# Attention stage of a two-layer diffusion trunk: four softmax divisions moved to another engine, one set of splits queued earlier, and the closing of a head placed between its transposes

## The chip, the cores and the metric

The kernel runs on one core of one Trainium2 chip. A core has four compute engines that the text names by short names: PE (TensorE, matrix products and transposes), DVE (VectorE), ACT (ScalarE) and POOL (GpSimd); PEld is PE's weight load, SP is the engine whose queue issues most of the DMA transfers. Each engine works through its own instructions in the order in which they stand, and waits at an instruction until the semaphores that it names have come. The metric is the device time of one execution in microseconds (us), the median over several executions; lower is better.

## The reference

The reference is a trunk of two layers over 1024 latent tokens and 256 context tokens, with 1024 channels. The part that matters here is layer 0, whose mixer has two groups of heads side by side: eight attention heads (two key/value heads, head size 64) and four HGRN heads (a gated linear recurrence in both directions). In short:

```
def attend(q, k, v):                       # per block of queries
    s = einsum("bqhgd,bkhd->bhgqk", q, k) * ATTN_SCALE
    p = softmax(s, axis=-1)
    return einsum("bhgqk,bkhd->bqhgd", p, v)
# latent queries: keys = 256 context + 1024 latent; context queries: the 256 context keys only
y = concat([attention heads, rms_norm(hgrn out) * silu(gate)], -1) @ w_out
x = x + g1 * rms_norm(y, norm_post_mix)
```

After it come the first ConvFFN, the second layer (neighbourhood attention) and the second ConvFFN; none of them is touched by the change.

## The kernel before, in words

The whole program is one list of instructions for each engine. Within the attention stage (`even_attention`, L1110) the order on every engine, SP included, is the order in which the code issues the work.

**Blocks, pairs and steps.** Queries are taken in five blocks of 256: block 0 is the context (`blocks` in `even_attention`), blocks 1 to 4 are the latent tokens. A pair is one block and one of eight heads, so there are 40 pairs: 0 to 7 for the context, 8 to 39 for the latent tokens. Each pair has two query tiles of 128. The loop at L1359 makes 88 steps `s`; the text calls a step even or odd by `s`. For the pair p a tile's scores are made in steps 2p and 2p+1, its exponential and its division one step later, its transposes in steps 2p+4 and 2p+5, its product with the values in steps 2p+6 and 2p+7, and its closing (`finish`) in step 2p+7. So in one step several pairs are at work, each at another place.

**One step on the engines.** PE makes the scores into the PSUM tile `a_s` (one buffer); DVE copies them, negated, into `l_p` with the row's minimum (L1179; `c_p` for the context); ACT takes the exponential in place and sums it (L1186). The division is DVE's reciprocal `rl` (L1191) and a multiplication by it on POOL (L1192). Then the probabilities are transposed on PE into `a_pt` (two buffers, `tp`), five key tiles to a step, in three pieces: two of 128x512 and a last one of 128x256. From each piece ACT makes the high half `a_ph` (L1213) and DVE the low half `a_pl` (L1214). PE multiplies both halves with the values into `a_pv` (one buffer, ten products to a step). The closing adds the two halves of `a_pv`: ACT copies the upper one to `pv_t` (L1249), DVE adds the lower one into `a_oT` (L1251). The next pair's products go into the same `a_pv`, so they wait for that addition.

**Filler.** Beside this PE has the output projection (`project`, L1280), cut into parts of three products (`g_ps<-w_h,a_oh` and so on). The function `step(n)` gives out n parts; a step of the loop calls it twice, between the pieces of the transposes. Every part also issues one item of the list `late`: the squares and copies of a finished projection tile, its norm, its residual, its stores. A block's 32 parts may only be given out once `st["ready"]` has reached the block; otherwise `step` only issues a waiting item of `late`, and PE has no filler. A block needs its attention output and its four HGRN tiles split into high and low halves (`split`, L1238: ACT makes `a_oh`, POOL makes `a_ol`). The list `todo` holds those splits; the end of each step takes some of them, one and a third of what is there. `gated` (L1261) first gives out what is left of the previous block's parts.

**The HGRN tiles.** They were stored to memory (`hgd`) by POOL's queue and are read again by SP's queue into `a_g`, four transfers to a block. The read is issued at the closing of the head 5 of the same block, in the buffer `r0` or `r1`.

**The first values.** The context's pairs use other PSUM tiles for their product: `h_pd` for pairs 0 to 2, then `a_s` for pairs 1 and 3 where the stage's own PSUM pool is already open (only pair 3 meets this), `g_ps` for pairs 5 and 7, and `a_pv` for the others. `a_s` lies over the banks that `h_pd` had.

Of the kernel before, what the change touches and what calls it, by code (L numbers as in the profile page):

```python
# [20 lines left out]
P = 128  # L21
# [47 lines left out]
class Trunk:  # L69
# [1040 lines left out]
    def even_attention(self, gp, tp, pp1, sp, more):  # L1110
# [77 lines left out]
        def divide(i):  # L1188
            Pt, nm, nk = st["t", i]
            rl = self.small.tile([P, 1], F32, name="rl")  # L1190
            nc.vector.reciprocal(rl, st.pop(("l", i)))  # L1191
            nc.gpsimd.tensor_scalar(Pt[:, :nk], Pt[:, :nk], rl, None, op0=OP.mult)  # L1192

        def half_keys(pair, half):

# [21 lines left out]
        def values(pair, half):  # L1217
            b, h = pairs[pair]
            kts = half_keys(pair, half)
            if half == 0:  # L1220
                pp = more.get("pp")
                if not pp:
                    st["pv"] = pp1.tile([P, 2, 5, 32], F32, name=f"h_pd{pair % 2}", bufs=1).rearrange("p a b c -> p (a b c)")
                elif pair in (1, 3):
                    st["pv"] = pp.tile([P, NT * P], F32, name="a_s", bufs=1)[:, :512]
                elif pair in (5, 7):
                    st["pv"] = gp.tile([P, 512], F32, name="g_ps")
                else:
                    st["pv"] = pp.tile([P, 512], F32, name="a_pv", bufs=1)
            pv, g = st["pv"], h // (AQ // AKV)  # L1230
            last = not half_keys(pair, 1) if half == 0 else True
            for j, kt in enumerate(kts):
                v = V2[keys(b)[0] // P + kt][:, g * P:(g + 1) * P]
                for x in range(2):
                    self.mm(pv[:, :QB], v, st["p", half][x][:, j], half == 0 and j == 0 and x == 0,
                            last and j == len(kts) - 1 and x == 1)
# [6 lines left out]
        def finish(pair):  # L1243
            b, h = pairs[pair]
            pv = st["pv"]
            if h % 2 == 0:
                st["oT"] = sp.tile([P, QB], F32, name="a_oT", bufs=2)
            t = pv_t[64:128]
            nc.scalar.copy(t, pv[64:128, :QB])  # L1249
            r = 64 * (h % 2)  # L1250
            nc.vector.tensor_tensor(out=st["oT"][r:r + 64], in0=pv[0:64, :QB], in1=t, op=OP.add)  # L1251
            if h % 2 == 1:
                todo.append(lambda oT=st["oT"]: split(b, h // 2, oT))
            if h == AQ - 3:
                g = st["g", b] = self.wp.tile([P, BH, QB], F32, name="a_g", tag=f"r{b % 2}")
                for k in range(BH):
                    nc.sync.dma_start(g[:, k, :], self.hgd[k][:, blocks[b][0]:blocks[b][0] + QB])
            if h == AQ - 1:
                todo.extend(lambda k=k: gated(b, k) for k in range(BH))

        def gated(b, k):  # L1261

            step(32 * b - at[0])
            split(b, BH + k, st["g", b][:, k, :])
            if k == BH - 1:
                st["ready"] = b

        def squares(y, ms):
            junk = sp.tile([P, 512], BF16, name="yjunk", bufs=1)
# [76 lines left out]
        load_values(NT - 2, NT)  # L1346
        load_q(2)
        load_ctx_keys(1)
        yield
        later = [lambda: load_keys(0, 0), lambda: load_keys(0, 1), lambda: load_values(0, NT - 2), lambda: load_keys(1, 0),  # L1350
                 lambda: load_keys(1, 1)] + [lambda m=m: load_w(m) for m in range(4)]
        for s in range(N + 8):
# [17 lines left out]
            step(1)  # L1370
            next(t, None)
            step(1)
            next(t, None)
            if 0 <= s - 1 < N:
                divide(s - 1)
            if 0 <= pair - 3 < len(pairs) and half == 1:
                finish(pair - 3)
            for _ in range(min(len(todo), 1 + len(todo) // 3)):
                todo.pop(0)()
            yield  # L1380
# [1590 lines left out]
```

## Time and profile before

| | |
|---|---|
| median of 3 executions | 3265.8 us (3262.59 to 3266.71) |
| profiled execution: its own time | 3258.97 us |
| profiled execution: span from first to last instruction | 3257.1 us |
| mean granted TensorE clock | 0.978 |
| PE busy over the span | 3065.0 us, 94% |
| DVE, ACT, POOL busy over the span | 66%, 46%, 48% |
| attention stage, latent scores to last transposes | about 640 to 990 us of the span |

The stage that the change touches is a ninth of the span. The shares over the whole span say little about it; what counts there is where PE stands idle inside a step, and which engine's instruction ends that idle time. A view by windows gives the busy time of each engine in a stretch; the timeline gives single instructions with the idle time before them in brackets and the instruction that ended it.

### The profile page before, as it was taken

Reading aid. Unit: us, or ns where it says so; the run is one execution under the profiler, and the core shown is the slowest. Engines: PE = TensorE matmul, PEld = TensorE weight load, DVE = VectorE, ACT = ScalarE, POOL = GpSimd, SP = SyncE. Lnnn points to the kernel's source line nnn. Section 1 sums busy time; section 2 is a strip of 40 time slices with the busy share of each in tenths; the row PEclk is TensorE's granted clock in tenths of the full one; section 3 lists DMA queues with packets and bytes.
Section 4 is the critical chain, followed back from the end, with each engine's and each line's share of the span. In section 5 each row is a group of like instructions: output and inputs, shape, how many; then the busy total and the mean of one; then the engine's idle time right before and its main releaser. Section 6 shows DMA issues by size and latency. Waiting matters only on the chain.

```text
span 3257.1 us, 48812 instructions
## 1 busy us (share of the span) xinstructions
PE 3065.0 (94%) x18161; PEld 2538.8 (78%) x18161; DVE 2147.4 (66%) x3619; ACT 1508.0 (46%) x2705; POOL 1576.6 (48%) x1165
## 2 busy tenths in 40 slices
PE   7989999789998899999999989999998989999999
PEld 4766777578876688888888768898986768888787
DVE  4556666677775787787678752577775464555787
ACT  3432332466665444334344442566665533443444
POOL 1130111377774677776600111677765367777300
PEclk8999999899999999999999989999998989999999
DMA  7734111711114344434365763222224212222755
GB/s 263 239 95 138 46 36 36 265 37 58 59 59 150 100 153 142 146 138 153 137 241 195 240 212 124 59 62 62 64 78 160 88 69 80 79 90 84 249 198 187
DMA packets 217142, 412.93 MB, mean 127 GB/s; under 512 B 25776, under 2 KB 87744, under 8 KB 216904
## 3 DMA queue, kind: packets, MB, share of 16 engines
q1 hardware_dynamic: 207208, 376.24, 34.5%
q0 software_dynamic: 9696, 33.57, 2.7%
q8 instruction: 143, 2.34, 0.3%
q14 instruction: 95, 0.78, 0.1%
HBM read 322.67 MB, written 87.44 MB: 126 GB/s over the span
## 4 chain that ended last, share of the span: by engine, by line
PE 76%; DVE 11%; issue 4%; ACT 3%; DMA 3%; POOL 2%; SPq 0%; POOLq 0%; ACTq 0%; DVEq 0%
PE g_ps L140 20%; PE u_g L140 14%; PE d_ps L140 12%; PE u_v L140 10%; PE u_pc L140 3%; PE a_pv L140 2%; PE c_pv L140 2%; PE c_s L140 2%; PE c_pt L2595 2%; PE a_pt L1212 2%; DVE a_pl L1214 1%; PE o_ps L140 1%; PE a_s L140 1%; DMA d_rawB<-in_w_down 1%; ACT a_ph L1213 1%
## 5 line engine op out<-in xcount | busy, mean ns | idle before, releaser
L148 POOL TENSOR_TENSOR rs_r<-rs_e,mhalf 128x1 f32<-128x1 f32 (+3 forms) x102 | 83.9, 824 | 833.6 <-DVE rs_e L147 466.2
L140 PE MATMUL d_ps<-d_Bl,d_Ah 128*128 128x512 f32 x704 | 276.5, 393 | 2.8 <-DVE d_Bl L1978 2.2
L2578 POOL TENSOR_SCALAR c_p<-c_p,rl 128x640 f32<-128x640 f32 (+1 forms) x128 | 232.6, 1818 | 94.6 <-DVE rl L2577 62.9
L140 PE MATMUL d_ps<-d_Bh,d_Ah 128*128 128x512 f32 x704 | 275.7, 392 | 2.4 <-ACT d_Ah L1977 1.4
L140 PE MATMUL d_ps<-d_Bh,d_Al 128*128 128x512 f32 x704 | 275.6, 391 | 1.5 <-DVE d_Al L1978 1.5
L140 PE MATMUL g_ps<-xh,w_hi 128*128 128x512 f32 (+1 forms) x640 | 256.7, 401 | 8.7 <-DVE hq L826 6.6
L1192 POOL TENSOR_SCALAR l_p<-l_p,rl 128x1280 f32<-128x1280 f32 x64 | 225.6, 3525 | 55.0 <-DVE rl L1191 48.8
L140 PE MATMUL g_ps<-xh,w_lo 128*128 128x512 f32 (+1 forms) x640 | 237.9, 372 | 1.2 <-POOL w_lo L2478 1.2
L140 PE MATMUL g_ps<-xl,w_hi 128*128 128x512 f32 (+1 forms) x640 | 237.7, 371 | 0.0
L1214 DVE TENSOR_TENSOR a_pl<-a_pt,a_ph 128x512 fp32r<-128x512 f32 (+1 forms) x200 | 119.0, 603 | 86.8 <-ACT a_ph L1213 86.3
L1653 DVE TENSOR_TENSOR f_u<-u_v,f_p 128x512 f32<-128x512 f32 x88 | 60.5, 687 | 156.6 <-PE u_v L140 156.6
L365 DVE CUSTOM_DVE_ANT_0 m_raw<-m_raw,c_row 128x512 f32<-128x512 f32 x128 | 147.0, 1158 | 24.8 <-DMA m_raw<-in_w_mod 24.8
L140 PEld LDWEIGHTS d_ps<-d_Bl,d_Ah 128*128 128x128 f32 x704 | 132.8, 189 | 34.2 <-DVE d_Bl L1978 5.5
L140 PEld LDWEIGHTS d_ps<-d_Bh,d_Ah 128*128 128x128 f32 x704 | 132.8, 189 | 31.9 <-ACT d_Ah L1977 2.6
L1639 POOL TENSOR_TENSOR w_S4l<-w_s,w_S4h 128x512 fp32r<-128x512 f32 x44 | 57.4, 1303 | 205.2 <-ACT w_S4h L1638 205.2
L140 PEld LDWEIGHTS d_ps<-d_Bh,d_Al 128*128 128x128 f32 x704 | 132.9, 189 | 30.1 <-DVE d_Al L1978 2.8
L2598 DVE TENSOR_TENSOR c_pl<-c_pt,c_ph 128x256 fp32r<-128x256 f32 (+1 forms) x256 | 113.1, 470 | 59.9 <-ACT c_ph L2597 58.7
L1213 ACT CAST a_ph<-a_pt 128x512 fp32r<-128x512 f32 (+1 forms) x200 | 101.9, 518 | 108.4 <-PE a_pt L1212 108.3
L140 PE MATMUL g_ps<-w_hi,xh 128*128 128x512 f32 (+1 forms) x368 | 143.4, 390 | 6.0 <-DVE xh L2352 3.4
L140 PEld LDWEIGHTS g_ps<-xh,w_hi 128*128 128x128 f32 x640 | 121.7, 190 | 27.8 <-issue 7.6
L140 PE MATMUL g_ps<-w_lo,xh 128*128 128x512 f32 (+1 forms) x368 | 138.2, 376 | 3.7 <-DVE w_lo L2339 2.6
L2597 ACT CAST c_ph<-c_pt 128x256 fp32r<-128x256 f32 (+1 forms) x256 | 98.4, 414 | 91.4 <-PE c_pt L2595 89.2
(602 smaller groups left out, 10018.6 us busy)
## 6 DMA issues: line engine op xcount, KB each, us to landing
w_raw<-in_w_up SPq DMA_DIRECT2D x88, 512.0 KB
d_rawA<-actd SPq DMA_DIRECT2D x77, 512.0 KB
d_rawB<-in_w_down SPq DMA_DIRECT2D x74, 512.0 KB
m_raw<-in_w_mod SPq DMA_DIRECT2D x128, 256.0 KB
m_raw<-in_w_mod SPq DMA_DIRECT2D x48, 512.0 KB
actd<-f_t SPq DMA_DIRECT2D x22, 640.0 KB
actd<-f_t SPq DMA_DIRECT2D x22, 512.0 KB
vcd<-cv_st POOLq DMA_DIRECT2D x20, 512.0 KB, 2.9
```

Source lines behind the costliest of these rows:

```text
L140: return self.nc.tensor.matmul(out, lhsT, rhs, start=start, stop=stop, skip_group_check=True, **k)
L148: nc.gpsimd.tensor_tensor(out=r[:p, :n], in0=e[:p, :n], in1=self.mhalf[:p, :n], op=OP.pow)
L365: nc.vector.tensor_tensor_reduce(out=w, in0=w, in1=halves[1][n % 2], scale=1.0, scalar=0.0, op0=OP.mult, op1=OP.add, accum_out=acc[:, k, o ...
L1192: nc.gpsimd.tensor_scalar(Pt[:, :nk], Pt[:, :nk], rl, None, op0=OP.mult)
L1212: nc.tensor.transpose(pt[:, m, qt * P:(qt + 1) * P], Pt[:, kts[j + m] * P:(kts[j + m] + 1) * P], self.ident)
L1213: nc.scalar.copy(ph[:, j:j + n], pt[:, :n])
L1214: nc.vector.tensor_tensor(out=pl[:, j:j + n], in0=pt[:, :n], in1=ph[:, j:j + n].bitcast(F32), op=OP.subtract)
L1653: nc.vector.tensor_tensor(out=out, in0=x, in1=y, op=OP.add)
L2578: nc.gpsimd.tensor_scalar(Pt[:, :n], Pt[:, :n], rl, None, op0=OP.mult)
L2595: nc.tensor.transpose(pt[:, j, :], Pt[:, (src + j) * P:(src + j + 1) * P], self.ident)
L2597: nc.scalar.copy(vap(ph, o, dims), pt[:, :cnt])
L2598: nc.vector.tensor_tensor(out=vap(pl, o, dims), in0=pt[:, :cnt], in1=vap(ph, o, dims).bitcast(F32), op=OP.subtract)
```

## The change

Four things are edited, all in `even_attention`.

1. In `divide`, the odd query tiles of pairs 8 to 11 (tile numbers 17, 19, 21 and 23) are multiplied by `rl` on ACT; the even ones stay on POOL.
2. In `values`, pair 3 uses `a_pv` as pair 4 does, and no longer `a_s`.
3. The HGRN tiles of a block are read one block earlier (`load_gated`): the context's before the loop, the block b+1's at the closing of head 5 of block b. For the context, the four HGRN splits are queued at the closing of head 4 instead of head 7. `ready` is set by an item of its own at the end of `todo`.
4. In the loop, `finish` comes after the second piece of the transposes and the filler behind it, before the third piece and the division; it came after both.

```diff
@@ divide
-            nc.gpsimd.tensor_scalar(Pt[:, :nk], Pt[:, :nk], rl, None, op0=OP.mult)
+            if 2 * AQ <= i < 3 * AQ and i % 2:
+                nc.scalar.mul(Pt[:, :nk], Pt[:, :nk], rl)
+            else:
+                nc.gpsimd.tensor_scalar(Pt[:, :nk], Pt[:, :nk], rl, None, op0=OP.mult)
@@ values
-                pp = more.get("pp")
-                if not pp:
+                if "pp" not in more:
...
-                elif pair in (1, 3):
-                    st["pv"] = pp.tile([P, NT * P], F32, name="a_s", bufs=1)[:, :512]
                 elif pair in (5, 7):
                     st["pv"] = gp.tile([P, 512], F32, name="g_ps")
                 else:
-                    st["pv"] = pp.tile([P, 512], F32, name="a_pv", bufs=1)
+                    st["pv"] = more["pp"].tile([P, 512], F32, name="a_pv", bufs=1)
@@ finish, load_gated, gated
             if h == AQ - 3:
+                load_gated(b + 1)
+            if (b, h) == (0, AQ - 4):
+                todo.extend(lambda k=k: gated(b, k) for k in range(BH))
+            if h == AQ - 1:
+                if b:
+                    todo.extend(lambda k=k: gated(b, k) for k in range(BH))
+                todo.append(lambda: st.update(ready=b))
+
+        def load_gated(b):
+            if b < len(blocks):
                 g = st["g", b] = self.wp.tile([P, BH, QB], F32, name="a_g", tag=f"r{b % 2}")
                 for k in range(BH):
                     nc.sync.dma_start(g[:, k, :], self.hgd[k][:, blocks[b][0]:blocks[b][0] + QB])
-            if h == AQ - 1:
-                todo.extend(lambda k=k: gated(b, k) for k in range(BH))
...
             split(b, BH + k, st["g", b][:, k, :])
-            if k == BH - 1:
-                st["ready"] = b
@@ before the loop
         load_ctx_keys(1)
+        load_gated(0)
         yield
@@ the loop
             step(1)
+            if 0 <= pair - 3 < len(pairs) and half == 1:
+                finish(pair - 3)
             next(t, None)
             if 0 <= s - 1 < N:
                 divide(s - 1)
-            if 0 <= pair - 3 < len(pairs) and half == 1:
-                finish(pair - 3)
```

The order of the engines shows how the instructions move. The first place is DVE in an odd latent step (the closing's step); `l_p,nm` is the copy of the scores, its second row reads the minimum. Before:

```order
L1214 TENSOR_TENSOR a_pl_7112<-a_pt,a_ph_7111 128x512 x2
L1214 TENSOR_TENSOR a_pl_7112<-a_pt,a_ph_7111 128x256
L1191 RECIPROCAL rl<-l 128x1
L1251 TENSOR_TENSOR a_oT<-a_pv,pv_t 64x256
L1179 ISA l_p,nm<-a_s,zeros 128x1280
```

The same place in the changed kernel:

```order
L1217 TENSOR_TENSOR a_pl_7123<-a_pt,a_ph_7122 128x512 x2
L1251 TENSOR_TENSOR a_oT<-a_pv,pv_t 64x256
L1217 TENSOR_TENSOR a_pl_7123<-a_pt,a_ph_7122 128x256
L1191 RECIPROCAL rl<-l 128x1
L1179 ISA l_p,nm<-a_s,zeros 128x1280
```

The addition into `a_oT` has moved ahead of the third low half and of the reciprocal; on ACT `pv_t` has moved in the same way ahead of the third high half.

The second place is ACT in the steps 20 to 22, which have no filler. Before:

```order
L1186 ACTIVATE l_p,l<-l_p,nm 128x1280
L1213 CAST a_ph_6851<-a_pt 128x512 x2
L1213 CAST a_ph_6851<-a_pt 128x256
L1186 ACTIVATE l_p,l<-l_p,nm 128x1280
L1213 CAST a_ph_6887<-a_pt 128x512 x2
L1213 CAST a_ph_6887<-a_pt 128x256
L1249 COPY pv_t<-g_ps 64x256
L1240 CAST a_oh<-a_oT 128x256
L1240 CAST a_oh<-a_g 128x256
L1186 ACTIVATE l_p,l<-l_p,nm 128x1280
```

The same place in the changed kernel:

```order
L1186 ACTIVATE l_p,l<-l_p,nm 128x1280
L1216 CAST a_ph_6872<-a_pt 128x512 x2
L1216 CAST a_ph_6872<-a_pt 128x256
L1193 ACTIVATE l_p<-l_p,rl 128x1280
L1186 ACTIVATE l_p,l<-l_p,nm 128x1280
L1216 CAST a_ph_6908<-a_pt 128x512 x2
L1249 COPY pv_t<-g_ps 64x256
L1216 CAST a_ph_6908<-a_pt 128x256
L1240 CAST a_oh<-a_oT 128x256
L1186 ACTIVATE l_p,l<-l_p,nm 128x1280
```

A multiplication by `rl` (L1193) stands between the third high half and the next exponential in the even step, and the split of an HGRN tile (`a_oh<-a_g`) has left the place.

The third place is DVE where the first finished projection tile of the context is normed (`y<-y,rs_r,gate`) and gets its residual (`y<-y,y_x`). Before, in an even step:

```order
L1214 TENSOR_TENSOR a_pl_7643<-a_pt,a_ph_7642 128x512
L424 SCALAR_TENSOR_TENSOR y<-y,rs_r,gate 128x1024
L1214 TENSOR_TENSOR a_pl_7643<-a_pt,a_ph_7642 128x512
L1307 TENSOR_TENSOR y<-y,y_x 128x1024
L1214 TENSOR_TENSOR a_pl_7643<-a_pt,a_ph_7642 128x256
L1191 RECIPROCAL rl<-l 128x1
```

In the changed kernel, one step earlier and so in an odd step:

```order
L1217 TENSOR_TENSOR a_pl_7588<-a_pt,a_ph_7587 128x512
L424 SCALAR_TENSOR_TENSOR y<-y,rs_r,gate 128x1024
L1217 TENSOR_TENSOR a_pl_7588<-a_pt,a_ph_7587 128x512
L1313 TENSOR_TENSOR y<-y,y_x 128x1024
L1251 TENSOR_TENSOR a_oT<-a_pv,pv_t 64x256
L1217 TENSOR_TENSOR a_pl_7588<-a_pt,a_ph_7587 128x256
L1191 RECIPROCAL rl<-l 128x1
```

The two operations on `y` now stand ahead of a closing. For the second tile of the context and for all later blocks the norm stays in an even step, as before.

## The prediction

> **What bounds the kernel now.** I read first the view by windows, to see where PE stands idle in the attention stage, then the list of waits for who ends that idle time, then the timeline of single steps. One row, the latent steps of the first block:
>
> ```profile
> 672.00:741.00 69.00, 66.43 (x429) 57.76 (x428) 50.75 (x95) 45.27 (x85) 50.91 (x22) 1.00 0.14 43
> ```
>
> The columns are the window, its length, the busy time of PE, PEld, DVE, ACT and POOL, the granted clock and the DMA share. Here, in the stage's steady part, PE is busy 96%, DVE 74%, ACT 66%, POOL 74%: PE sets the pace, and only its own short waits can be won. The waits between 672 and 991 us (total, times, longest):
>
> ```profile
> PE a_pv L140 <- DVE a_oT L1251: 12.9, 28, 1.4
> PE a_pt L1212 <- DVE a_pl L1214: 9.8, 12, 1.0
> ```
>
> The largest is the wait of the next pair's values product for the closing of the pair before. Two steps of PE, an even one and an odd one, show what it costs:
>
> ```profile
> 691.35 1.17 PE L140 MATMUL a_s<-K,a_q 128*128 128x512 f32 x4
> 692.36 0.40 PE L140 MATMUL a_s<-K_1c,a_q 128*128 128x256 f32 x2
> 693.03 0.39 PE L140 MATMUL a_pv<-a_ph,V 128*128 128x256 f32 x1 [0.28 <-DVE a_oT L1251]
> ...
> 696.75 1.17 PE L140 MATMUL a_s<-K,a_q 128*128 128x512 f32 x4
> 697.75 0.40 PE L140 MATMUL a_s<-K_1c,a_q 128*128 128x256 f32 x2
> 697.99 0.28 PE L140 MATMUL a_pv<-a_ph,V 128*128 128x256 f32 x1
> ...
> 701.61 1.17 PE L140 MATMUL a_s<-K,a_q 128*128 128x512 f32 x4
> ```
>
> The even step takes 696.75 - 691.35 = 5.40 us, the odd one 701.61 - 696.75 = 4.86, with the same work. So the wait, listed as 0.28, costs 0.54: the pipeline is refilled too.
>
> **The change, part by part.**
>
> **(a) The closing between the transposes.** What stands ahead of `a_oT` in the odd step, on DVE and on ACT:
>
> ```profile
> 691.33 1.14 DVE L1214 TENSOR_TENSOR a_pl<-a_pt,a_ph 128x512 fp32r<-128x512 f32 x2 [0.39 <-ACT a_ph L1213]
> 692.38 0.15 DVE L1191 RECIPROCAL rl<-l 128x1 f32<-128x1 f32 x1
> 692.56 0.42 DVE L1251 TENSOR_TENSOR a_oT<-a_pv,pv_t 64x256 f32<-64x256 f32 x1
> 693.01 1.49 DVE L1179 CUSTOM_DVE_ANT_0 l_p<-a_s,zeros 128x1280 f32<-128x1280 f32 x1
> ```
>
> ```profile
> 690.71 0.59 ACT L1213 CAST a_ph<-a_pt 128x512 fp32r<-128x512 f32 x1 [0.49 <-PE a_pt L1212]
> 691.63 0.37 ACT L1213 CAST a_ph<-a_pt 128x256 fp32r<-128x256 f32 x1 [0.34 <-PE a_pt L1212]
> 692.03 0.37 ACT L1249 COPY pv_t<-a_pv 64x256 f32<-64x256 f32 x1
> ```
>
> In the new order `pv_t` follows the second high half at 691.30 and ends at 691.67. On DVE the second low half ends about 692.05 (the pair of 1.14 less the third of 0.42), so `a_oT` runs from there to 692.47 in place of 692.98. PE would come to its product at 692.36 + 0.24 = 692.60, the 0.24 read from the odd step. The wait is gone, with 0.13 to spare. What becomes late: the third high half by 0.37, the third low half and `rl` by 0.42. The next copy of scores is not later, since the same instructions precede it, and its end at 694.50 is 2.2 ahead of the next scores at 696.75; the third low half is needed two steps on. POOL's division begins 0.42 later, and the transposes use it more than a step later.
>
> Of the 28 waits 22 are of this plain kind (0.26 to 0.29): 22 x 0.54 = 11.9. Three have ACT's scaling of a finished row ahead of the closing, and the last three, in steps without scores, wait longer:
>
> ```profile
> 787.00 1.15 ACT L1315 ACTIVATE y_x<-y,rs_r 128x1024 f32<-128x1024 f32 x1
> 789.44 0.38 PE L140 MATMUL a_pv<-a_ph,V 128*128 128x256 f32 x1 [0.88 <-DVE a_oT L1251]
> 971.98 0.39 PE L140 MATMUL a_pv<-a_ph,V 128*128 128x256 f32 x1 [1.44 <-DVE a_oT L1251]
> ```
>
> There `a_oT` comes 0.5 earlier and part of the wait stays: 6 x 0.5 = 3.0. Together **-14.9**. Bounds: -17 if these six go nearly whole; -5 if the 0.13 to spare are eaten and most waits form again at a third of their cost.
>
> **(b) The filler one step earlier.** The context's blocks of filler start in step 23, not 24, since `ready` comes one step sooner. The amount of filler is the same; the burst in step 37 gives two parts less. But the finished tile's norm, residual and squares move into odd steps, ahead of a closing. Their rows, in the even step where they are now, and what they cost there:
>
> ```profile
> 727.50 1.19 PE L140 MATMUL a_s<-K,a_q 128*128 128x512 f32 x4
> ...
> 727.00 1.79 DVE L424 SCALAR_TENSOR_TENSOR y<-y,rs_r,gate 128x1024 f32<-128x1024 f32 x1
> 729.32 1.21 DVE L1307 TENSOR_TENSOR y<-y,y_x 128x1024 f32<-128x1024 f32 x1
> ...
> 732.99 0.44 PE L1212 MATMUL a_pt<-ident,l_p 128*128 128x128 f32 x2 [0.59 <-DVE a_pl L1214]
> 737.33 0.64 ACT L1271 ACTIVATE yjunk<-y 128x512 bf16<-128x512 f32 x1
> ```
>
> Now the wait is 0.59, with its refill about 0.8. In the odd step `a_oT` stands behind the residual: it would end at 729.32 + 1.21 + 0.42 = 730.95 on this scale, while PE's next scores begin at 727.50 and its product could start 1.25 behind them (692.60 - 691.35), at 728.75: a wait of 2.2, with refill 2.4. The squares (two of 0.64 on ACT, 1.3) do the same two steps on, estimated at 0.9, and a small sum before them at 0.4. Net 2.4 + 0.9 + 0.4 - 0.8 = **+2.9**; bounds 0 and +4. Later blocks keep the norm in an even step, by the order shown.
>
> **(c) Pair 3's values in `a_pv`.**
>
> ```profile
> 634.77 0.55 PE L140 MATMUL a_s<-a_ph,V 128*128 128x256 f32 x1 [2.33 <-DVE a_oT L1251]
> ```
>
> `a_s` lies on the bank of pair 2's product, so this product waits 2.33 for pair 2's closing. `a_pv` lies elsewhere; the product then needs pair 3's low half only. But pair 4's product goes into the same `a_pv` two steps on and must wait for pair 3's closing, which it does not today, so part of the wait moves there. I take **-1.0**, between 0 and -2.3.
>
> ```profile
> 630.00:635.00 5.00, 2.15 (x12) 1.54 (x13) 3.75 (x14) 2.97 (x10) 4.88 (x7) 0.97 0.67 202
> 635.00:640.00 5.00, 4.40 (x22) 3.71 (x23) 2.10 (x10) 2.28 (x7) 2.84 (x4) 0.69 0.57 175
> ```
>
> Behind this idle time the granted clock is 0.69. The Trainium skill (TensorE: Matmul & The Clock Gate, Part 1: The HAM clock gate) puts the clock at half after an idle window of some 3.4 us and full again after as long a busy one. By that rule a shorter gap could save up to 4.40 x (1 - 0.69) = 1.4 more, which would make the sum below -12.0; the window's phase is unknown, and the sum leaves it out.
>
> **(d) Splits and divisions in the steps without filler.** The context's HGRN splits stand on ACT ahead of an exponential; these steps are 5.3 and 4.7 us long (from score to score below), the one before them 3.8:
>
> ```profile
> 662.83 0.40 ACT L1240 CAST a_oh<-a_g 128x256 fp32r<-128x256 f32 x1
> 666.72 0.71 ACT L1240 CAST a_oh<-a_g 128x256 fp32r<-128x256 f32 x2
> ...
> 657.05 1.18 PE L140 MATMUL a_s<-K,a_q 128*128 128x512 f32 x4
> 660.85 1.18 PE L140 MATMUL a_s<-K,a_q 128*128 128x512 f32 x4
> 666.17 1.18 PE L140 MATMUL a_s<-K,a_q 128*128 128x512 f32 x4
> 670.86 1.17 PE L140 MATMUL a_s<-K,a_q 128*128 128x512 f32 x4
> ```
>
> Queued from head five on they fall in context steps where ACT idles, so **-1.4** (with the fourth of 0.4; bounds 0 and -2.4, both steps down to 3.8).
>
> A division on ACT is not in the trace. The nearest row is the exponential in the same tile, 1.36:
>
> ```profile
> 651.28 10.64 POOL L1192 TENSOR_SCALAR l_p<-l_p,rl 128x1280 f32<-128x1280 f32 x3
> 652.95 1.36 ACT L1186 ACTIVATE l_p<-l_p,nm 128x1280 f32<-128x1280 f32 x1 [1.17 <-DVE nm L1179]
> ```
>
> It must also wait for `rl`, which ends 0.53 behind the third high half (692.53 against 692.00 in the rows above), and the next exponential is queued behind it, then the next step's high halves, for which DVE and the third transposes wait. So 1.9 each, four times: 7.6 if nothing hides it. POOL's three divisions end to end show it full there, but PE nowhere waits for a latent division, so what POOL is spared gains nothing by itself; the lower bound is 0 (POOL as the limit is a rival below). The first two (tiles 17 and 19) fall where ACT idles, as in the 1.17 above; 21 and 23 come on a full ACT. I take half, **+3.8**.
>
> **(e) SP's queue.** The context's four reads now stand among the HGRN stage's loads. Three wait for a buffer that is free before the next load; the fourth waits for head 3's store and stands ahead of a weight load:
>
> ```profile
> 564.07 0.63 POOL L1107 DMA_DIRECT2D hgd<-h_o  x1 [0.30 <-POOL h_o L1105]
> 567.50 0.33 SPq L224 DMA_DIRECT2D m_raw<-in_w_mod  x1
> DMA to landing us min/median/max: 2.1/2.4/4.7
> L140 PE MATMUL g_ps<-m_raw,csil x64: 591/593/617, 584.5 to 597.9; 128*32 128x512 f32 x64
> ```
>
> The store lands between 566.2 and 568.8, the load was issued at 567.50 and is used from 584.5 on: **0**, at most 1.3 without that cover.
>
> **Sum:** -14.9 + 2.9 - 1.0 - 1.4 + 3.8 = -10.6. The profiled execution took 3258.97, so 3248.4; the median shown lies 6.8 above that execution, so **3255** as a median. Everything behind the stage follows from its end (output projection, then the FFN) and moves with it.
>
> **The rivals.**
>
> *The wait forms again.* The 0.13 to spare in (a) is small; with -5 there the sum is -0.7, about 3265, no change. For it: the closing still needs the second low half. Against: DVE's steps repeat to a few hundredths.
>
> *ACT's queue is full.* None of the divisions is hidden: +7.6 for +3.8, sum -6.8, 3259. For it: order, one engine, a wait inside. Against: only two of four are in such steps.
>
> *POOL was the limit at the start.* If the back-to-back divisions held the steps without filler, sparing them takes 3.8 off the sum at least: 3251. Against: no PE wait names POOL there.
>
> *The third piece becomes the bound (slower).* Place: the odd step's last low half and `rl`, 0.42 later each pair. If the next minimum slips by that and the scores wait for it, each of 32 pairs loses 0.42 (+13.4) and (a) gains nothing: 13.4 + 2.9 - 1.0 - 1.4 + 3.8 = +17.7, 3283. It decides once the slip passes the 2.2 us of slack read above.
>
> **How the numbers follow.** Differences under 0.2% (6.5 us) can't be told from no change here. The forecast has 0.58 (0.54 faster, 0.04 same), the wait formed again 0.17 (0.16 same, 0.01 faster), ACT's queue 0.09 (0.05 faster, 0.04 same), POOL 0.06, slower 0.10. So faster 0.66, same 0.24, slower 0.10. The forecast's own range is 3249 to 3261; with the first rivals and the bounds the range is 3247 to 3267, which leaves out most of the slower case.
>
> **What would show it.** Right: the wait `a_pv <- a_oT` falls from 28 to fewer than ten, even and odd steps both take 4.86 us, and a block of sixteen steps is 3.5 us shorter. In the first latent block one wait of about 2 us behind the residual. Around 655 to 675 us ACT without idle time and transposes that wait longer than 1.0. Wrong: steps still alternating, scores waiting for `nm`, or the stage's gain missing from the end of the program.

## The result, and the profile after

The changed kernel takes 3256.9 us as the median of 10 executions (3248.14 to 3260.79); the kernel before, on the same chip, 3265.8 (10 executions, 3260.37 to 3270.09). The ratio is 0.9972 with a 95% interval of 0.9963 to 0.9982: faster by 9 us, which is 0.28%, with 0.18% to 0.37% by the interval. The forecast was 3255, between 3247 and 3267. The profiled execution took 3256.98 (span 3255.2).

PE's waits in the changed kernel, in the same window as before (total, times, longest):

```profile
PE a_pt L1215 <- DVE a_pl L1217: 9.1, 13, 1.0
PE a_pv L140 <- DVE a_oT L1251: 6.7, 8, 1.6
```

The second row was 12.9 us in 28 waits. An even step, the odd one behind it and the start of the next, from PE's timeline:

```profile
696.32 1.17 PE L140 MATMUL a_s<-K,a_q 128*128 128x512 f32 x4
...
701.31 1.17 PE L140 MATMUL a_s<-K,a_q 128*128 128x512 f32 x4
...
706.14 1.17 PE L140 MATMUL a_s<-K,a_q 128*128 128x512 f32 x4
707.15 0.40 PE L140 MATMUL a_s<-K_1c,a_q 128*128 128x256 f32 x2
707.39 0.32 PE L140 MATMUL a_pv<-a_ph,V 128*128 128x256 f32 x1
```

The steps take 4.99 and 4.83; the alternation of 5.40 and 4.86 is gone. DVE in the closing's step:

```profile
706.12 0.69 DVE L1217 TENSOR_TENSOR a_pl<-a_pt,a_ph 128x512 fp32r<-128x512 f32 x1 [0.39 <-ACT a_ph L1216]
706.85 0.42 DVE L1251 TENSOR_TENSOR a_oT<-a_pv,pv_t 64x256 f32<-64x256 f32 x1
```

ACT in the same step:

```profile
706.11 0.37 ACT L1249 COPY pv_t<-a_pv 64x256 f32<-64x256 f32 x1
706.51 0.37 ACT L1216 CAST a_ph<-a_pt 128x256 fp32r<-128x256 f32 x1
```

`a_oT` ends at 707.27 and the product begins at 707.39: 0.12 to spare, where 0.13 was forecast.

**The stage as a whole.** I measure it from DVE's first copy of context scores to the start of PE's last product of the output projection. In the timeline of before these are the rows

```profile
607.36 0.42 DVE L1179 CUSTOM_DVE_ANT_0 c_p<-g_ps,zeros 128x256 f32<-128x256 f32 x1
...
1020.82 0.40 PE L140 MATMUL g_ps<-w_h,a_ol 128*128 128x512 f32 x1
```

and in that of the change

```profile
610.53 0.42 DVE L1179 CUSTOM_DVE_ANT_0 c_p<-g_ps,zeros 128x256 f32<-128x256 f32 x1
...
1013.32 0.40 PE L140 MATMUL g_ps<-w_h,a_ol 128*128 128x512 f32 x1
```

so 413.5 and 402.8: the stage is 10.7 us shorter, the forecast's sum being 10.6. In these two executions the whole program is only 2.0 shorter (3258.97 against 3256.98). Two places outside the stage account for most of that. The stage begins 3.2 later though everything up to 567 us came 0.8 earlier; PE stood still there for nothing that the profile shows:

```profile
592.51 0.45 PE L140 MATMUL h_pa<-hQ,hKM 128*32 128x32 f32 x30 [0.36 <-ACT hKM L880]
596.22 0.22 PE L140 MATMUL h_pa<-hQ,hKM 128*32 128x32 f32 x1 [3.26 <-issue]
```

And from 1816 to 1939 us of the span the gain shrinks from 5.8 to 2.6. That is a stretch of products whose weights are being loaded by DMA meanwhile. Its row in the view by windows (columns as in the prediction, GB/s last), before:

```profile
1816.00:1940.00 124.00, 109.93 (x452) 84.60 (x451) 81.50 (x116) 58.02 (x80) 21.09 (x35) 0.93 0.83 271
```

The same row of the change:

```profile
1816.00:1940.00 124.00, 107.22 (x437) 81.44 (x436) 80.33 (x114) 58.03 (x80) 20.53 (x34) 0.93 0.81 260
```

The one profile of before was quick there: all the 13 other profiles of this study take 0.6 to 5.9 longer over that stretch, whatever their stage does. So the stage's length is what the experiments are compared by, and the program's median beside it; one execution of e8, which took 4345.6 us at a granted clock of 0.649, is left out of its median.

### The profile page after: what moved, and what is told of

The parts are those of the page before. It is cut to its first block, busy times and chain, and to the rows that moved or that the text cites. A ratio compares the mean times of both kernels' runs of the same rounds, so it can differ in the third digit from the quotient of the medians.

```text
span 3255.2 us, 48808 instructions
## 1 busy us (share of the span) xinstructions
PE 3063.5 (94%) x18161; PEld 2537.5 (78%) x18161; DVE 2147.3 (66%) x3619; ACT 1511.7 (46%) x2709; POOL 1563.5 (48%) x1161
## 3 DMA queue, kind: packets, MB, share of 16 engines
q8 instruction: 142, 2.33, 0.3%
## 4 chain that ended last, share of the span: by engine, by line
PE 76%; DVE 10%; DMA 4%; issue 4%; ACT 4%; POOL 2%; SPq 0%; POOLq 0%; ACTq 0%; DVEq 0%
PE g_ps L140 21%; PE u_g L140 13%; PE d_ps L140 12%; PE u_v L140 10%; PE u_pc L140 3%; PE a_pv L140 2%; PE c_pv L140 2%; PE c_s L140 2%; PE c_pt L2602 2%; PE a_pt L1215 2%; PE a_s L140 2%; PE o_ps L140 1%; DVE a_pl L1217 1%; DMA d_rawB<-in_w_down 1%; DMA m_raw<-in_w_mod 1%
## 5 line engine op out<-in xcount | busy, mean ns | idle before, releaser
L1195 POOL TENSOR_SCALAR l_p<-l_p,rl 128x1280 f32<-128x1280 f32 x60 | 211.5, 3524 | 63.2 <-DVE rl L1191 47.4
```

## The experiments

The stage in parts, in us: steps 0 to 8 and 8 to 16 (context), 16 to 27 (first latent steps), 27 to 39, 39 to 79, and from the last copy of scores to the end. Each part runs from one copy of scores on DVE to another. Where parts have nothing different in them the later ones repeat to 0.2 us; the first three do not: two profiles of the change (the change, e5) are 1.3 apart in the stage, two of the divisions alone (e4, e11) 0.5. Except for the change, e5, e4 and e11, each kernel has one profile. (The expectations of e1 to e8 name stages 0.2 to 0.3 shorter, since they end one product earlier.)

| kernel | 0-8 | 8-16 | 16-27 | 27-39 | 39-79 | end | stage | median, us (executions) | ratio to before, 95% |
|---|---|---|---|---|---|---|---|---|---|
| before | 20.3 | 14.7 | 45.7 | 64.4 | 214.6 | 53.8 | 413.5 | 3265.8 (10) | |
| the change | 20.2 | 15.1 | 47.0 | 63.1 | 204.9 | 52.4 | 402.8 | 3256.9 (10) | 0.9963 to 0.9982 |
| e5, the change again | 20.4 | 16.2 | 47.1 | 63.1 | 205.0 | 52.4 | 404.1 | 3257.1 (11) | 0.9967 to 0.9985 |
| e1, closing only | 20.7 | 14.8 | 44.6 | 61.7 | 204.6 | 52.4 | 398.7 | 3246.9 (5) | 0.9928 to 0.9956 |
| e2, no division on ACT | 20.3 | 15.5 | 44.8 | 63.0 | 204.7 | 52.4 | 400.7 | 3248.6 (5) | 0.9941 to 0.9966 |
| e3, late read | 20.6 | 16.1 | 50.6 | 63.1 | 204.9 | 52.4 | 407.7 | 3256.8 (11) | 0.9969 to 0.9987 |
| e4, divisions only | 19.7 | 14.5 | 52.7 | 64.5 | 214.5 | 53.8 | 419.6 | 3271.6 (11) | 1.0011 to 1.0029 |
| e6, filler later | 20.1 | 15.5 | 44.6 | 61.6 | 204.7 | 52.4 | 398.9 | 3248.2 (6) | 0.9936 to 0.9964 |
| e7, pair 3 back | 20.2 | 14.3 | 47.2 | 63.0 | 204.7 | 52.4 | 401.9 | 3251.6 (5) | 0.9946 to 0.9972 |
| e8, ready first | 20.3 | 14.5 | 44.9 | 59.9 | 203.4 | 52.4 | 395.5 | 3246.4 (4) | 0.9929 to 0.9955 |
| e9, addition early | 20.2 | 14.4 | 45.9 | 63.6 | 211.3 | 53.5 | 408.9 | 3256.4 (1) | |
| e10, copy early | 20.2 | 14.7 | 45.7 | 65.1 | 217.6 | 54.2 | 417.5 | 3260.2 (1) | |
| e11, divisions again | 20.3 | 14.7 | 51.3 | 64.5 | 214.6 | 53.8 | 419.2 | 3269.8 (1) | |
| e12, residual on POOL | 21.5 | 14.9 | 45.2 | 61.3 | 203.0 | 52.5 | 398.5 | 3249.1 (4) | 0.9931 to 0.9966 |

### The closing between the transposes: e1, e9, e10

e1 is the kernel before with the fourth edit alone:

```diff
             step(1)
+            if 0 <= pair - 3 < len(pairs) and half == 1:
+                finish(pair - 3)
             next(t, None)
             if 0 <= s - 1 < N:
                 divide(s - 1)
-            if 0 <= pair - 3 < len(pairs) and half == 1:
-                finish(pair - 3)
```

> The kernel before with the fourth edit alone (the closing between the transposes). The stage is measured in the profile from DVE's first copy of context scores to PE's last product of the output projection: 413.2 us before, 402.6 with the whole change. Theory (the closing carries the gain): the plain waits of 0.26 to 0.29 behind a_oT go, even and odd steps take 4.86 us alike, a block of sixteen steps gets 3.5 to 3.9 shorter, the stage 13 to 15 shorter, the program about 13 us (0.4%). Rival (the wait forms again elsewhere): 5 us or less, with the steps still at 5.2 or more somewhere. Second rival (the other edits carry part of the gain): less than 10.7.

Measured: stage 398.7, 14.8 shorter than before; a block of sixteen steps 82.2 for 86.1. The waits of e1 between 672 and 991 us have one row for the closing:

```profile
PE a_pv L140 <- DVE a_oT L1251: 4.2, 6, 0.9
```

The starts of three steps in its timeline are 4.89 and 4.87 apart:

```profile
689.90 1.18 PE L140 MATMUL a_s<-K,a_q 128*128 128x512 f32 x4
...
694.79 1.17 PE L140 MATMUL a_s<-K,a_q 128*128 128x512 f32 x4
...
699.66 1.17 PE L140 MATMUL a_s<-K,a_q 128*128 128x512 f32 x4
```

What is left are the six waits that the prediction had said would only shrink. The program is 19 us faster (14 to 24 by the interval), at 3246.9 us the quickest beside e8. So one edit carries more than the whole gain, and the other three together cost 4.1 us of the stage and 10 us of the median.

e9 and e10 take the edit's two halves apart. In e9 the addition moves ahead on DVE, and the copy stays behind the third high half on ACT (the third piece is issued in two parts, its low half by the added `next`):

```diff
                 nc.scalar.copy(ph[:, j:j + n], pt[:, :n])
+                if j == 4:
+                    yield
...
-            if 0 <= s - 1 < N:
-                divide(s - 1)
             if 0 <= pair - 3 < len(pairs) and half == 1:
                 finish(pair - 3)
+            next(t, None)
+            if 0 <= s - 1 < N:
+                divide(s - 1)
```

> The kernel before with half of the fourth edit: a_oT goes ahead of the third low half and rl on DVE, but pv_t stays behind the third high half on ACT. The stage takes 413.5 us before and 398.7 with the whole fourth edit. Theory (both queues had to give way, and only 0.13 us were to spare): a_oT now waits on DVE for pv_t, ends about 0.37 later than with the whole edit, the wait behind it is still in the list at about 0.1 to 0.2, and the stage gains 3 to 6 of the 14.8. Rival (DVE's queue alone was the cause): 12 us or more, no plain wait left.

In e10 the copy leaves `finish` and moves ahead on ACT, and the addition stays where it was on DVE:

```diff
             step(1)
+            if 0 <= pair - 3 < len(pairs) and half == 1:
+                nc.scalar.copy(pv_t[64:128], st["pv"][64:128, :QB])
             next(t, None)
...
-            nc.scalar.copy(t, pv[64:128, :QB])
```

> The kernel before with the other half of the fourth edit: pv_t goes ahead of the third high half on ACT, a_oT stays behind the third low half and rl on DVE. Theory (a_oT stands in DVE's queue until rl is done, whatever pv_t does): the 28 waits behind a_oT stay at 0.26 to 0.29 and the stage within 1 us of 413.5. Rival (pv_t was what a_oT waited for): a gain of 5 us or more.

DVE's timeline in e9, at the closing:

```profile
691.62 0.42 DVE L1253 TENSOR_TENSOR a_oT<-a_pv,pv_t 64x256 f32<-64x256 f32 x1 [0.40 <-ACT pv_t L1251]
```

PE's product behind it in e9:

```profile
690.55 1.19 PE L140 MATMUL a_s<-K,a_q 128*128 128x512 f32 x4
691.57 0.40 PE L140 MATMUL a_s<-K_1c,a_q 128*128 128x256 f32 x2
692.10 0.39 PE L140 MATMUL a_pv<-a_ph,V 128*128 128x256 f32 x1
```

DVE's timeline in e10, at a closing:

```profile
688.77 1.22 DVE L1214 TENSOR_TENSOR a_pl<-a_pt,a_ph 128x512 fp32r<-128x512 f32 x2 [0.39 <-ACT a_ph L1213]
689.90 0.15 DVE L1191 RECIPROCAL rl<-l 128x1 f32<-128x1 f32 x1
690.09 0.42 DVE L1250 TENSOR_TENSOR a_oT<-a_pv,pv_t 64x256 f32<-64x256 f32 x1
```

The second and the third high half on ACT in e10, with the copy between them:

```profile
688.15 0.59 ACT L1213 CAST a_ph<-a_pt 128x512 fp32r<-128x512 f32 x1 [0.49 <-PE a_pt L1212]
...
689.16 0.37 ACT L1213 CAST a_ph<-a_pt 128x256 fp32r<-128x256 f32 x1
```

And the product behind it in e10:

```profile
690.65 0.35 PE L140 MATMUL a_pv<-a_ph,V 128*128 128x256 f32 x1 [0.43 <-DVE a_oT L1250]
```

In e9 the addition waits 0.40 for the copy, the product comes 1.55 behind the scores in place of 1.25, and the stage gains 4.6, as expected (3 to 6). One thing came otherwise: waits of 0.1 to 0.2 were expected in the list, and it has none of the plain kind, only six long ones (6.1 us in total). Yet a pair takes 10.61 us there for 10.28 in e1 and 10.77 before: this delay of the product is seen in the length of the steps and not in the list. In e10 I was wrong: no change was expected, and the stage is 4.0 *longer* than before. With the copy ahead of it the third high half starts 1.01 behind the second (689.16 - 688.15), for 0.92 before (691.63 - 690.71); most of the copy's 0.37 fits into the 0.34 for which ACT had waited there. The third low half, `rl` and then `a_oT`, all still in the old order on DVE, come some 0.1 later too: `a_oT` starts 1.30 behind the scores, for 1.21 before. The wait grows from 0.28 to 0.43, and a pair takes 10.91 us for 10.77. An operation that nobody was waiting for had been put ahead of one that DVE's queue did wait for. Only both moves together pay in full: 4.6 and -4.0 apart, 14.8 together.

### The filler one step earlier: e6 against e2

e6 is the change with all divisions on POOL (e2, below) and `ready` of the context one step later, as before:

```diff
-                todo.append(lambda: st.update(ready=b))
+                todo.append(lambda: todo.append(lambda: st.update(ready=b)) if b == 0 else st.update(ready=b))
```

> The changed kernel with all divisions on POOL (e2, stage 400.4 us) and the context's filler one step later, so that its first norm, residual and squares come in even steps as before. Theory (the norm in an odd step delays the closing behind it): the waits of 1.6 and 0.8 behind a_oT in the first latent block go and the stage gets 1.3 us shorter (predicted 2.9 net; e1 and e2 differ by 1.3 between steps 27 and 39). Rival (the earlier filler gains as much as the norm costs, since two parts fewer fall into the burst): the stage within 0.5 us of 400.4.

Measured: 1.7 shorter than e2, of which 1.4 in steps 27 to 39. PE's waits of e2 between 720 and 740 us

```profile
726.93 0.39 PE L140 MATMUL a_pv<-a_ph,V 128*128 128x256 f32 x1 [1.62 <-DVE a_oT L1248]
...
737.67 0.39 PE L140 MATMUL a_pv<-a_ph,V 128*128 128x256 f32 x1 [0.79 <-DVE a_oT L1248]
```

are gone in e6; in their place it has the one wait of 0.44 for low halves. The first is the closing behind the residual, the second the copy behind the squares. In the changed kernel they read 1.61 and 0.80.

### Pair 3's product: e7 against e2

```diff
+                elif pair == 3:
+                    st["pv"] = more["pp"].tile([P, NT * P], F32, name="a_s", bufs=1)[:, :512]
```

> The changed kernel with all divisions on POOL (e2, stage 400.4 us) and pair 3's product back in a_s. In the changed kernel pair 3's product waits 0.5 in place of 2.3, but pair 4's product waits 1.5 to 1.9 for pair 3's closing and the clock in 640 to 645 us is 0.55 to 0.66. Theory (the wait only moved): pair 3's product waits 2 us or more again, pair 4's not at all, and context and first latent steps take the same time within 0.5 us. Predicted was a gain of 1.0 by the edit, so 1.0 longer here. Rival (the moved wait costs more, by the clock): 0.5 to 1 us shorter here.

First the changed kernel: pair 3's product, which waited 2.33 before, and pair 4's.

```profile
636.05 0.38 PE L140 MATMUL a_pv<-a_ph,V 128*128 128x256 f32 x1 [0.53 <-ACT a_ph L1216]
636.77 0.39 PE L140 MATMUL a_pv<-a_pl,V 128*128 128x256 f32 x1 [0.34 <-DVE a_pl L1217]
...
641.50 0.55 PE L140 MATMUL a_pv<-a_ph,V 128*128 128x256 f32 x1 [1.91 <-DVE a_oT L1251]
```

The wait has moved two steps on, as the prediction said, but not in part: 2.33 became 0.53 + 0.34 + 1.91. In e7 pair 3's product waits 2.19 and pair 4's not at all, and steps 8 to 16 take 14.3 for 15.5. Over all profiles the kernels with `a_s` there need 14.3 to 14.9, those with `a_pv` 15.1 to 16.2: the edit costs about 1 us. So in the context the rival held. Yet e7's stage is 1.2 longer than e2's, because steps 16 to 27 lost 2.4. There its clock fell. Three windows of e6, which up to step 22 differs from e7 only in pair 3's place and begins step 16 within 0.3 us of it (the granted clock is the third number from the end):

```profile
640.00:645.00 5.00, 4.07 (x22) 3.13 (x20) 3.83 (x10) 4.47 (x11) 3.46 (x5) 0.94 1.01 368
...
650.00:655.00 5.00, 3.24 (x17) 2.43 (x16) 3.37 (x7) 3.27 (x6) 5.00 (x3) 1.00 0.30 93
655.00:660.00 5.00, 3.46 (x23) 2.80 (x23) 3.63 (x7) 3.31 (x7) 5.00 (x4) 1.00 0.02 3
```

The same windows of e7:

```profile
640.00:645.00 5.00, 3.69 (x20) 2.57 (x18) 3.96 (x11) 4.48 (x12) 4.38 (x6) 1.00 1.02 375
...
650.00:655.00 5.00, 3.41 (x13) 2.71 (x12) 2.31 (x6) 2.92 (x5) 5.00 (x4) 0.69 0.45 153
655.00:660.00 5.00, 4.40 (x18) 3.71 (x18) 3.38 (x6) 2.31 (x4) 4.17 (x3) 0.50 0.00 0
```

The drop is not the edit's: from 650 us to the end of step 22 e2, e6 and e7 issue the same instructions, and e2 and e6 have 1.00 there; so has e1, which has pair 3 in `a_s` as e7 has and takes 44.6 for steps 16 to 27. The Trainium skill (TensorE: Matmul & The Clock Gate, Part 1: The HAM clock gate) says that the window of the gate runs freely and does not start with the kernel, so that the same code meets it at another phase in each execution. The trace agrees as far as it goes: the same order had 1.00 and 0.50 in the same steps.

### Divisions on ACT: e2, e4, e11

e2 is the change without the first edit, as shown; e4 is the kernel before with the first edit alone, so the reverse of this diff; e11 is e4's kernel once more:

```diff
-            if 2 * AQ <= i < 3 * AQ and i % 2:
-                nc.scalar.mul(Pt[:, :nk], Pt[:, :nk], rl)
-            else:
-                nc.gpsimd.tensor_scalar(Pt[:, :nk], Pt[:, :nk], rl, None, op0=OP.mult)
+            nc.gpsimd.tensor_scalar(Pt[:, :nk], Pt[:, :nk], rl, None, op0=OP.mult)
```

> The changed kernel with all divisions on POOL. Theory (the divisions on ACT lengthen the first latent steps): the steps 20 to 26, at 4.6 and 5.5 us in turn in the changed kernel, fall back, no transposes wait 1 us or more there, and the stage is 2 to 4 us shorter than the 402.6 of the changed kernel. Rival (POOL was the limit there and the divisions relieve it): transposes wait for POOL's l_p between 650 and 690 us, and the stage is 2 us or more longer than 402.6.

> The kernel before with the first edit alone (four divisions on ACT). Theory: the steps 18 to 25 together are 2 to 5 us longer (predicted 3.8, between 0 and 7.6), the stage 2 to 5 us longer than 413.2, the program the same within what can be measured. Rival (POOL was the limit): the stage 1 us or more shorter. Second rival (ACT's queue is full there): 6 to 8 us longer.

> The kernel before with four divisions on ACT, once more. Its first profile (e4) had the steps 17 to 27 7.0 us longer than before, with a granted clock of 0.75 to 0.89 between 640 and 670, where the changed kernel, with the same divisions, lost 2.2 and had 1.00 from 650 on. Theory (2 us are the divisions, the rest is where the clock's drops happen to fall): the second profile has other drops, and the loss follows them, between 2 and 7. Rival (all of it is ACT's full queue, with the splits in the same steps): again 7.0 within 0.5, with drops at the same places.

A division as it stands on ACT in the changed kernel, ahead of the next exponential:

```profile
662.09 1.36 ACT L1193 ACTIVATE l_p<-l_p,rl 128x1280 f32<-128x1280 f32 x1 [0.62 <-DVE rl L1191]
663.36 1.34 ACT L1186 ACTIVATE l_p<-l_p,nm 128x1280 f32<-128x1280 f32 x1
```

PE's waits behind two such divisions:

```profile
666.04 0.44 PE L1215 MATMUL a_pt<-ident,l_p 128*128 128x128 f32 x2 [2.94 <-DVE a_pl L1217]
...
676.16 0.44 PE L1215 MATMUL a_pt<-ident,l_p 128*128 128x128 f32 x2 [0.37 <-DVE a_pl L1217]
```

The mechanism is the predicted one: 1.36 and, in three of the four, a wait of 0.62, so 1.98, then the exponential, then the high halves for which the third transposes wait. In e2 no transposes wait over 1.3 there (none of 1 us or more had been expected), and steps 16 to 27 take 44.8 for 47.0: the four divisions cost 2.2 us. Most of it lies behind the second of them: steps 21 and 22 take 10.1 us for 8.6 in e2, the two steps behind the third and behind the fourth some 0.5 more each. POOL was not the limit; in e2 and e6 it is full again (5.00 of 5.00 in e6's windows above) and transposes wait 0.5 for it, once. Without the other edits the same divisions cost much more, 7.0 (e4, where 2 to 5 were expected) and 5.6 (e11). PE's waits in e11:

```profile
661.96 0.69 PE L1215 MATMUL a_pt<-ident,l_p 128*128 128x128 f32 x2 [2.94 <-DVE a_pl L1217]
...
674.10 0.44 PE L1215 MATMUL a_pt<-ident,l_p 128*128 128x128 f32 x2 [2.38 <-DVE a_pl L1217]
```

The two windows of e11 in which they lie:

```profile
660.00:665.00 5.00, 3.04 (x10) 2.66 (x11) 2.28 (x6) 3.34 (x9) 1.25 (x1) 0.67 0.00 0
...
675.00:680.00 5.00, 4.66 (x23) 4.09 (x23) 2.43 (x6) 2.68 (x5) 4.22 (x2) 0.66 0.02 5
```

The wait of 2.38 stands where the change has filler already and waits 0.37. That the third edit's earlier filler pays back part of the first here is likely and not shown, since the second and fourth edits differ as well. And behind both long waits the clock falls: in e11 to 0.67 and 0.66, in e4 to between 0.80 and 0.86 and to 0.66; e4 has drops at 650 and 655 as well (0.77, 0.89). So neither of my two theories holds alone. Steps 21 to 26 take the same 35.1 us in both, 5.6 more than before; e4's further loss lies in the steps 19 and 20, at its drops of 650 and 655. But the 5.6 are not the full queue alone. Step 21, with the wait of 2.94, takes 6.74 in both and 6.75 in e3, where the clock falls there too; in the change, with the same wait and a clock of 1.00, it takes 5.53. So 1.2 of the 5.6 come from the clock behind the first long wait. What it took behind the second is not known, and the queue itself costs at most some 4.4. The change's own steps lost to the clock as well in e3 (0.77 at 650, 0.66 at 655 and again at 665, behind a wait of 2.95; steps 16 to 27 take 50.6 for 47.0), but not in the two profiles of the change itself.

In the medians e2 is 8 us ahead of the change, by the ratios 6 with an uncertainty of about 5; the stage accounts for 2.2, and 5.8 where the clock fell (e3 less e2 in steps 16 to 27). The order holds over all kernels: with the closing moved, those with divisions on ACT have ratios of 0.9972 to 0.9978, those without 0.9942 to 0.9959. How often the clock falls was not measured, so it stays open what makes the divisions cost more in the medians than in the profiles.

### The reads of `a_g`, and PE's unexplained stop: e3, e5

```diff
-        load_gated(0)
         yield
-        later = [lambda: load_keys(0, 0), ...
+        later = [lambda: load_gated(0), lambda: load_keys(0, 0), ...
```

> The changed kernel with the context's four a_g reads issued behind the stage's first step, not among the HGRN stage's loads. In the changed kernel's profile PE stood 3.3 us at 592.9 for no semaphore, which moved the stage's start from 0.8 us early to 3.2 us late; a 16 KB block of the instruction queue arrived there at 593.8, where before one arrived at 590.0. Theory one (the early reads hold up SP's queue and so something that PE needs): without them the stage starts 0.5 to 1 us earlier than before, no such wait. Theory two (PE waits for its own instructions, whose transfer meets full DMA engines, by chance): the same wait can be there or not, whether the reads are early or late, and kernels without early reads show it too. The stage itself stays within 1 us of 402.6.

> The changed kernel once more, for a second profile of it beside kernels of the same hour. Theory (the 3.3 us that PE stood at 592.9 for no semaphore are a transfer of PE's own instructions among full DMA engines, and come by chance): the wait is gone or has another length, and the stage takes 402.6 us within 1. Rival (the early a_g reads or the order of the queue make it): the same wait at the same matmul, and the stage again starts 3 to 4 us later than in kernels without early reads.

SP's longest wait for a store in the changed kernel, between 555 and 612 us:

```profile
SPq L1267 <- DMA hgd<-h_o: 5.5, 1, 5.5
```

SP's issues there:

```profile
565.34 0.33 SPq L1267 DMA_DIRECT2D a_g<-hgd  x1
566.66 0.33 SPq L224 DMA_DIRECT2D m_raw<-in_w_mod  x1
```

SP stood 5.5 us at the fourth read, but the weight load behind it went at 566.66 for 567.50 before, which is only the general lead of 0.8: it had to wait for PE anyway. So the early reads cost nothing. The stop of 3.26 us is not theirs either: it is absent in e3, and also in e2, e5, e6 and e7, which read early, and there in e12, which does not (2.44 us, at the same matmul). e5's stage does start 4.0 us later than before's, as its rival had said, but e5 is that late already at 488 us, ahead of these reads. e5's stage is 1.3 longer than the change's first one, nearly all of it in the context, more than the 1 expected. What goes with it is a 16 KB transfer of the instruction queue. The DMA view between 588 and 593 us (packets, MB, share of 16 engines), before:

```profile
q1 hardware_dynamic: 468, 1.70, 96.8%
q8 instruction: 1, 0.02, 1.8%
```

In the change there is none in this window:

```profile
q1 hardware_dynamic: 470, 1.73, 97.9%
```

In the change that packet comes at 593.8, 15.8 us after the one before it, and PE goes on at 596.2. In e12 it is 15.4; in the 12 profiles without the stop 10.6 to 11.6. That PE waited for its own code is the likeliest reading, since the two come together in 2 of 14 and are missing together in 12; it is not shown, for the trace does not say whose code the packet holds. e3's stage is 4.9 longer than the change's for another reason: the clock between 650 and 670, told above, and a third profile of `a_pv` in the context (16.1).

### Two attempts at a faster kernel: e8, e12

Both start from e1. In e8 a block's filler is free at its first HGRN split, so that the burst of four parts and the two steps without filler disappear (first piece of the diff); in e12 the residual goes to POOL (second piece):

```diff
-            if k == BH - 1:
+            if k == 0:
                 st["ready"] = b
...
-late.append(lambda y=y, xt=xt: nc.vector.tensor_tensor(out=y, in0=y, in1=xt, op=OP.add))
+late.append(lambda y=y, xt=xt: nc.gpsimd.tensor_tensor(out=y, in0=y, in1=xt, op=OP.add))
```

> The closing between the transposes alone (e1, stage 398.5 us), and a block's filler set free at its first HGRN split, not at its last. In e1 a block has one step of 7.2 us with a burst of four parts and two behind it of 4.69 without filler, in which PE waits 1.02 each. Theory (the two steps without filler are what is left to win): the burst spreads over them, all plain steps take 4.86, each of four blocks gets about 2.0 shorter (7.2 - 4.86 less 2 x 0.17), the first latent block too has filler two steps sooner, and the stage is 7 to 9 us shorter than 398.5. Rival (PE has as much to do and the waits come again elsewhere): less than 2 us shorter.

> The closing between the transposes alone (e1, stage 398.7 us) with the residual of the finished projection tile (y + y_x, 1.21 us on DVE) on POOL. What is left in e1 are steps of 6.5 and 5.4 us around the norm, in which PE waits up to 1.0 for low halves that stand behind the norm and the residual on DVE. Theory (DVE bounds those steps): about 1 us less for each of ten tiles, 5 to 9 us shorter than e1. Rival (POOL, busy 82% there, answers too late, and the squares on ACT behind the residual hold the high halves): longer than e1 by 2 us or more.

e8's stage is 3.2 shorter than e1's, where 7 to 9 were expected, and e12's 0.2 shorter, where 5 to 9 were. In the program neither can be told from e1. One window of e1:

```profile
835.00:918.00 83.00, 79.65 (x521) 69.94 (x521) 64.24 (x122) 59.17 (x115) 68.52 (x34) 1.00 0.17 58
```

The same window of e8:

```profile
835.00:918.00 83.00, 80.81 (x526) 70.78 (x525) 66.30 (x122) 59.94 (x117) 69.01 (x34) 1.00 0.18 58
```

PE is busy 96% and 97%: with the closing's wait gone little idle time of PE is left, and filler that is moved takes its own time with it. My expectation for e8 had counted all that the step of 7.2 takes beyond 4.86 as won, and not that its burst is work. e12's 0.2 hides two things: from step 27 on, where the residuals are, it is 1.8 shorter than e1, and 1.6 longer ahead of that, where the two kernels have the same instructions.

## Why the prediction was right

The sum was right to 0.1 us in this pair of profiles, and by its large term. The last digit is luck: with e5 in place of the change's first profile the stage is 9.4 shorter. Each edit's share, taken along the chain before, e1, e6, e2, the change, against the prediction's steps:

| step of the prediction | forecast | measured | from |
|---|---|---|---|
| (a) closing | -14.9 | -14.8 | e1 less before |
| (c) pair 3, and the splits of (d) | -1.0 and -1.4 | +0.3 together | e6 less e1 |
| (b) filler one step earlier | +2.9 | +1.7 | e2 less e6 |
| (d) divisions on ACT | +3.8 | +2.1 | the change less e2 |
| sum | -10.6 | -10.7 | |

**(a)** held in every part: 22 plain waits gone, six shrunk, 0.12 to spare, a block 3.9 shorter (3.5 said). That each listed 0.28 costs 0.54 is confirmed by the steps, and e9 confirms that the margin is thin. Only the third high half is less late than said: it starts 1.01 behind the second (706.51 less 705.50 on ACT) for 0.92 before, so 0.09 later and not 0.37, since ACT had stood idle ahead of it.

**(b)** had the right mechanism and too large a size. The wait behind the residual is 1.61 for 2.2, since the norm there took 1.27 us and not 1.79, and two parts fewer in the burst may have given something back.

**(c)** failed in its sign. "Part of the wait moves there" was the step: all of it moved and more, and steps 8 to 16 are about 1 us longer (0.7 from e1 to e6, of which the first steps, that differ by chance, give 0.5 back in the table). The clock's drop moved with the wait (0.69 from 635 to 640 us before, 0.66 from 640 to 645 in the change), so the further 1.4 did not come either. **(d)** failed in the splits: steps 16 to 27 take 44.6 with them (e1) and 44.6 without (e6); what limits these steps is by PE's waits there the low halves on DVE, and not the splits in ACT's queue. The closing had already taken 1.1 off these steps (45.7 before). The divisions came within the bounds: three of the four take 1.98 of ACT (1.9 forecast), and 2.1 of 7.9 is not hidden, where half had been taken. But their places were wrong: the second (tile 19), put where ACT idles, cost 1.5, and tiles 21 and 23, put on a full ACT, some 0.5 each. By the medians all four cost about 6, with an uncertainty of 5, so their true size in the program is open. **(e)** was right at 0.

So four small terms were wrong by 1 to 2 us each, and their errors cancelled (forecast +4.3 together, measured +4.1). The step from profile to median was also helped by luck: I added 6.8 since before's profile lay below its median, which was right, for that profile was a quick one. Between 1816 and 1939 us the 13 others take 2.9 longer on average; the rest of the 6.8 is not explained.

**The rivals.** The wait did not form again. POOL was not the limit (e2 is faster than the change). The third piece did not become the bound: scores wait for `nm` nowhere behind 660 us. "ACT's queue is full" had 7.6 unhidden: with the other edits it is 2.1, and where the divisions stand alone (e4, e11) at most some 4.4 without the clock's part.

**What would show it** came as said: 8 waits in place of 28, one of about 2 us behind the residual, transposes over 1.0 in the first latent steps. But that last sign says little: before has four such waits there too, of 1.0 to 1.7, and only the one of 2.94 is new. ACT without idle time did not: it waits for `rl` in each division.

## What to carry to other kernels

A wait of PE that is listed as 0.28 us can cost 0.54 each time, and a delay that the list does not name 0.33 (e9): compare the length of steps, not the list of waits alone. When an operation is moved ahead, move what feeds it on every engine with it; half of the move was worth less than a third, or made it worse. And measure each edit of a bundle apart: here one edit was worth 19 us of the program, and the bundle 9.

## What the runs showed of the hardware that was not expected

PE stood still for 3.26 and 2.44 us at the same matmul in 2 of 14 profiles, each time with a 16 KB instruction packet that came 4 us late while the DMA engines were busy 97 to 103%; before, without a stop, they were as busy (97 to 101%). The Trainium skill (Runtime: NRT & Kernel Launch, Instruction fetch mechanics) says that an engine's code is fetched in blocks of 16 KB by a queue of its own, and that the cost of passing from block to block is mostly hidden. If the stop is such a fetch, which is not shown, it was hidden here 12 times of 14.

The granted clock fell to 0.50 to 0.80 for 5 to 15 us in some executions and not in others over the same steps, where PE is busy 65 to 73% of the time at full clock (e7 against e6, 650 to 665 us). It cost 2.4 us in e7 (against e2), and 3.6 in e3 (against the change): as much as any of the small edits was worth, in one profile and not in the next.
